# The last MLP of a hybrid trunk: down weights that change places in their buffers, a residual turned into the sums at the opening, and accumulators seeded from the sums

## The chip, the cores and the metric

The kernel runs on one core of a Trainium2 chip. Its metric is the device time in microseconds (us) of one execution, the median over several. A core has five engines with instruction queues of their own: TensorE (PE, with its weight loads PEld), VectorE (DVE), ScalarE (ACT), GpSimd (POOL) and SyncE (SP). SP and POOL here do little but issue transfers (DMA).

## The reference

A trunk of two layers on x of 512 tokens by 1024: each is a mixer and a squared-ReLU MLP, both behind an RMS norm. At the end stands one more RMS norm. The change lies in the second layer's MLP and the final norm:

```python
def rms_norm(x, gain):
    xf = x.astype(jnp.float32)
    y = xf * lax.rsqrt(jnp.mean(xf * xf, axis=-1, keepdims=True) + EPS)
    return (y * gain.astype(jnp.float32)).astype(x.dtype)
...
def sq_relu_mlp(xn, w_up, w_down):
    hid = jnp.square(jax.nn.relu(xn @ w_up))
    return hid @ w_down
```

w_up is 1024 x 4096, w_down 4096 x 1024, all in float32. The layer gives x + hid @ w_down; the kernel's output is the norm of that.

## The kernel before

**Layout.** The residual is kept transposed in xall: eight tiles xT of [128, 512], features on the partitions. Each float32 operand of a product is split in two parts of the matmul's rounded type: a high part `wh` (ACT, L104) and a low part `wl` (DVE, L107); a product is then three matmuls. Output of the down product has tokens on the partitions.

**The last MLP** is `mlp_last`. The 4096 hidden features are cut in eight blocks of 512. The first block's up product is made plainly by `up_first`, the last block's down product plainly by `row`. Between them run seven steps; step b makes the down product of block b and the up product of block b+1, each as a 2 x 2 block product with seven instead of eight multiplications. These need sums of weight quadrants and of operand quadrants, made by DVE. An up product is 24 matmuls of 128x256 (`up_product`, L1083), a down product 12 of 128x512 (`down_product`, L1094).

Five sums of down products are kept over all steps: S11, S12, SU and S21 are views of xall (1024 numbers per partition each), S5 is a tile of its own. A step computes in two-bank PSUM tiles d and e, and in four banks for the up products; results are added to the sums by DVE (L1117) or the sum is copied into the bank by ACT first (L1122) and the product accumulated on it.

**Weights of a step.** `fetch(b, name)` loads them: A1 and A2 (1 MB each, up), S1 (up, 512 KB), d11, d12, d22, dS1 and dS3 (down, 512 KB). SP issues the plain load (L1080, L134). S1, dS1, dS3 and A2 are sums of two quadrants: behind the plain load, POOL issues a second one that accumulates in flight (L1082, L1072). dS1 enters first through DVE's `d11 += ds1` at L1145, by which d11 becomes the sum for a later product; S1 through L1141.

The six 512 KB weights live in six buffers, all of the tag "comb". `step` calls `after(name)` where a weight has been used for the last time, and the next block's weight of the same name is fetched into the buffer that comes free; the names are released in the order d11, S1, d12, A1, dS3, dS1, A2, d22.

**The residual.** xall becomes the sums, so at the opening its content is written to DRAM (x_kept, 2 MB, L982). Step 0 is special ("opening"): it writes the sums rather than adding to them. In the last step, `at_the_end` reads x_kept back in four parts into freed buffers (L1222), and loads the last block's down weights as two 1 MB tiles. Then `residual(t, c)` turns 4 tiles on PE (L129), DVE adds them to a sum (L1253), ACT copies the result into an accumulator (L1257), and `row(t, c)` adds the last block's 12 matmuls (L1267), squares and sums on ACT (L1270), multiplies by the gain on DVE (L1271), and at c = 1 scales by the row's factor and writes out (L1279 to L1289).

**What sets the order.** The engines' order of instructions comes from a list scheduler in the framework, which also puts in the waits; an engine runs its list in order. SP's and POOL's lists are in order too.

Of the kernel before, what the change touches and what calls it, by code (L numbers as in the profile page):

```python
# [18 lines left out]
P = 128  # L19
D = 1024  # L20
# [30 lines left out]
def trunk_kernel(ctx: ExitStack, tc: tile.TileContext, t_in: dict, out: bass.AP):  # L51
# [7 lines left out]
    def uname(s):  # L59
        count[0] += 1  # L60
        return f"{s}_{count[0]}"
# [17 lines left out]
    def two_banks(tag):  # L79
        return psum["pool"].tile([P, 1024], F32, tag=f"ps_{tag}", bufs=1, name=uname("ps2"))  # L80
# [891 lines left out]
    def mlp_last(layer, nrm):  # L972
# [6 lines left out]
        fast = es.enter_context(tc.tile_pool(name=f"fast{layer}", bufs=1, reuse_waits="tile"))  # L979
        dram = es.enter_context(tc.tile_pool(name="spill", bufs=1, space=bass.MemoryType.DRAM))  # L980
        x_kept = dram.tile([P, ND, S], F32, name="x_kept")
        SP.dma_start(x_kept, xall)  # L982

# [6 lines left out]

        def comb():
            return fast.tile([P, 2 * S], F32, tag="comb", bufs=6, name=uname("comb"))

        def by_k(t, n):
            return t.rearrange("p (k n) -> p k n", k=n)
# [41 lines left out]
        def quadrants():  # L1037
            lead, trail = range(KH), range(KH, ND)
            quad["11"] = [nrm.parts[k][:, :, first] for k in lead]
            quad["21"] = [nrm.parts[k][:, :, first] for k in trail]  # L1040
            quad["22"] = [nrm.parts[k][:, :, second] for k in trail]
            t1, t2, t3, t4 = (by_k(comb(), KH) for _ in range(4))
# [12 lines left out]


        W = {}

# [45 lines left out]
        def step(b, q, r, after):  # L1104
            opening = b == 0
            (q11, q12), (q21, q22) = q

            def begun(src, total):
                if opening:
                    ACT.activation(total, src, AF.Copy)  # L1110
                    return two_banks("e")
# [7 lines left out]
            def onto(tag, total, a, parts):  # L1119
                t = two_banks(tag)  # L1120
                if not opening:
                    ACT.activation(t, total, AF.Copy)  # L1122
                down_product(t, a, parts, opening)
                ACT.activation(total, t, AF.Copy)
# [11 lines left out]
            down_product(d, d11, parts_of_quad(q11), True)  # L1136
            e = begun(d, S11)

# [3 lines left out]

            down_product(e, d12, parts_of_quad(q21), opening)
            add(S11, e)
# [9 lines left out]
            down_product(d, d11, parts_of_quad(q11, -1.0), False)  # L1154
            e = begun(d, S12)
            DVE.tensor_tensor(d12, d11, d12, ALU.add)
# [7 lines left out]

            down_product(e, d12, parts_of_quad(q22), opening)
            add(S12, e)
# [8 lines left out]
            down_product(d, ds3, parts_of_quad(q12), False)  # L1175
            if opening:
                ACT.activation(SU, d, AF.Copy)
            else:
                add(SU, d)
            after("dS3")  # L1180
# [8 lines left out]

            onto("e", S5, ds1, parts_of_quad(q22, -1.0))  # L1190
            after("dS1")
# [10 lines left out]
        quadrants()  # L1202
        NAMES = ("d11", "S1", "d12", "A1", "dS3", "dS1", "A2", "d22")
        for name in NAMES:
            fetch(0, name)

        kept, last = [], []

        def at_the_end(name):
            if name in ("A1", "A2"):  # L1210
                c = len(last)
                raw = load(w_dn[(NB - 1) * FB :, c * 512 : (c + 1) * 512].rearrange("(k p) n -> p k n", p=P), 4, 512)
                w = []
                for k in range(4):
                    parts = both_parts()
                    split(raw[:, k], parts[:, 0], parts[:, 1])
                    w.append((parts[:, 0], parts[:, 1]))
                last.append(w)
            elif len(kept) < ND // 2:
                t = by_k(comb(), 2)  # L1220
                i = 2 * len(kept)
                SP.dma_start(t, x_kept[:, i : i + 2])  # L1222
                kept.append(t)
            elif len(kept) == ND // 2:
                t = comb()
                SP.dma_start(t, t_in["fin_row"].to_broadcast([P, D]))
                DVE.tensor_scalar(t, t, -0.5, None, ALU.mult)
                kept.append(t)

        for b in range(NB - 1):  # L1230
            step(b, Q[b % 2], Q[(b + 1) % 2], (lambda name, b=b: fetch(b + 1, name)) if b < NB - 2 else at_the_end)


        q = Q[(NB - 1) % 2]
        DVE.tensor_tensor(S12, S12, S5, ALU.add)
        hid = {}
        for h in range(2):
            for th in range(2):
                hid[h, th] = parts_of_quad(q[h][th])
        DVE.tensor_tensor(S21, S21, SU, ALU.add)  # L1240
        DVE.tensor_tensor(SU, SU, S5, ALU.add)
        gain = kept.pop()
        place = {}
        stats = [sm(3) for _ in range(NT)]
        rows = {}

        def residual(t, c):
            src = (S11, S12, S21, SU)[2 * c + t // 2][:, t % 2 * 512 : (t % 2 + 1) * 512]
            p = bank("u")
            for j in range(4):  # L1250
                m = 4 * c + j
                tr(p[:, j * P : (j + 1) * P], kept[m // 2][:, m % 2, t * P : (t + 1) * P])
            DVE.tensor_tensor(src, p, src, ALU.subtract if c else ALU.add)  # L1253
            if t % 2 == 0:
                place["t"] = two_banks("ed"[t // 2])
            o = place["t"][:, t % 2 * 512 : (t % 2 + 1) * 512]
            ACT.activation(o, src, AF.Copy)  # L1257
            rows[t, c] = src, o

        def row(t, c):  # L1260
            y, o = rows[t, c]
            tk = slice(t % 2 * P, (t % 2 + 1) * P)
            for k in range(4):
# [6 lines left out]
            ACT.activation(sq, o, AF.Square, accum_out=stat[:, c : c + 1])  # L1270
            DVE.tensor_tensor(y, o, gain[:, c * 512 : (c + 1) * 512], ALU.mult)  # L1271
            part = stat[:, 2:3]
            if c == 0:
                DVE.tensor_scalar(part, stat[:, 0:1], 1.0 / D, EPS, ALU.mult, ALU.add)
                return
# [7 lines left out]
            y_0 = rows[t, 0][0]  # L1283
            for eng, queue, y_, cs in ((DVE, SP, y_0, slice(0, 512)), (ACT, ACT, y, slice(512, D))):
                if eng is ACT:
                    ACT.activation(y_, y_, AF.Copy, scale=r)
                else:
                    DVE.tensor_scalar(y_, y_, r, None, ALU.mult)
                queue.dma_start(out_t[:, cs], y_)  # L1289

        order = [(t, c) for c in range(2) for t in range(NT)]
        residual(*order[0])
        residual(*order[1])
        for i, tc_ in enumerate(order):
            if i + 2 < len(order):
                residual(*order[i + 2])
            row(*tc_)
        es.close()


# [547 lines left out]
```

## Time and profile before

| | us |
|---|---|
| median of 3 runs | 1097.58 |
| lowest, highest | 1096.39, 1097.94 |
| the profiled execution | 1098.03 |
| its span | 1096.3 |
| PE busy in it | 1067.1 (97%) |
| DVE busy | 871.5 (79%) |
| ACT busy | 625.7 (57%) |
| POOL busy | 75.9 (7%) |

The mean granted TensorE clock is 0.993. Times in the profile are counted from the span's start; `mlp_last`'s seven-product part fills it from about 762 us to the end. A row of the waits reads: engine and line that waited, engine and line waited for, total us, times, longest. A row of the timeline reads: start, duration, engine, line, operation, result and operands, count, and in brackets the idle time ahead of it with what ended it. A row of the windows reads: the stretch, its length, and for each engine the busy time with its count of instructions, then the granted clock, the DMA engines' share and GB/s. A row of the chain reads: start, duration, what.

### The profile page before, as it was taken

Reading aid. Unit: us, or ns where it says so; the run is one execution under the profiler, and the core shown is the slowest. Engines: PE = TensorE matmul, PEld = TensorE weight load, DVE = VectorE, ACT = ScalarE, POOL = GpSimd, SP = SyncE. Lnnn points to the kernel's source line nnn. Section 1 sums busy time; section 2 is a strip of 40 time slices with the busy share of each in tenths; the row PEclk is TensorE's granted clock in tenths of the full one; section 3 lists DMA queues with packets and bytes.
Section 4 is the critical chain, followed back from the end, with each engine's and each line's share of the span. In section 5 each row is a group of like instructions: output and inputs, shape, how many; then the busy total and the mean of one; then the engine's idle time right before and its main releaser. Section 6 shows DMA issues by size and latency. Waiting matters only on the chain.

```text
span 1096.3 us, 14765 instructions
## 1 busy us (share of the span) xinstructions
PE 1067.1 (97%) x5626; PEld 912.9 (83%) x5626; DVE 871.5 (79%) x1394; ACT 625.7 (57%) x1009; POOL 75.9 (7%) x100
## 2 busy tenths in 40 slices
PE   9999999999999999999999999999899999999976
PEld 7888888888888888888788888888789889889864
DVE  7899968987887887877694696497978988988873
ACT  7667654554453453455446545655667767667554
POOL 7210002000000000000000000001011011011000
PEclk9999999999999999999999999999999999999989
DMA  7311232232332332323213212158568679669412
GB/s 221 89 49 39 78 115 78 66 127 77 116 115 77 115 116 77 115 78 115 87 39 115 76 40 78 39 169 273 131 158 224 144 177 239 149 160 234 134 57 77
DMA packets 103430, 127.87 MB, mean 117 GB/s; under 512 B 8416, under 2 KB 74464, under 8 KB 103232
## 3 DMA queue, kind: packets, MB, share of 16 engines
q1 hardware_dynamic: 90064, 110.42, 31.5%
q0 software_dynamic: 11200, 14.68, 8.1%
q10 hardware_dynamic: 2096, 1.84, 0.5%
q8 instruction: 44, 0.72, 0.3%
q14 instruction: 26, 0.21, 0.1%
HBM read 122.47 MB, written 4.19 MB: 116 GB/s over the span
## 4 chain that ended last, share of the span: by engine, by line
PE 78%; DMA 11%; DVE 6%; ACT 2%; issue 2%; POOL 0%; DVEq 0%; SPq 0%; POOLq 0%; ACTq 0%
PE ps L112 15%; PE ps L114 15%; PE ps L113 15%; DMA comb<-in_mlp_w_down_dram 9%; PE ps L891 8%; PE ps L1092 6%; PE ps L1101 5%; PE ps L892 4%; DVE wl L107 2%; PE ps L1267 2%; PE ps L129 2%; PE ps L1492 1%; PE ps L408 1%; DMA wraw<-in_mlp_w_down_dram 1%; PE ps L1619 1%
## 5 line engine op out<-in xcount | busy, mean ns | idle before, releaser
L104 ACT ACTIVATE wh<-wraw 128x1024 fp32r<-128x1024 f32 x139 | 146.4, 1056 | 156.5 <-PE ps L113 76.4
L112 PE MATMUL ps<-set,wh 128*128 128x512 f32 x536 | 209.1, 391 | 0.5 <-ACT set L1661 0.3
L113 PE MATMUL ps<-set,wh 128*128 128x512 f32 x536 | 209.2, 391 | 0.0
L114 PE MATMUL ps<-set,wl 128*128 128x512 f32 x536 | 208.8, 390 | 0.0
L107 DVE TENSOR_TENSOR wl<-wraw,wh 128x1024 fp32r<-128x1024 f32 x139 | 169.4, 1220 | 33.2 <-ACT wh L104 33.0
L1101 PE MATMUL ps<-wh,set 128*128 128x512 f32 x392 | 129.7, 392 | 0.7 <-ACT wh L104 0.7
L104 ACT ACTIVATE wh<-comb 128x1024 fp32r<-128x1024 f32 x77 | 81.6, 1059 | 77.0 <-PE ps L891 40.9
L107 DVE TENSOR_TENSOR wl<-comb,wh 128x1024 fp32r<-128x1024 f32 x77 | 93.8, 1218 | 32.5 <-ACT wh L104 32.2
L112 PEld LDWEIGHTS ps<-set,wh 128*128 128x128 f32 x536 | 100.6, 188 | 22.3 <-ACT wh L104 1.0
L114 PEld LDWEIGHTS ps<-set,wl 128*128 128x128 f32 x536 | 100.6, 188 | 21.5 <-DVE wl L107 0.4
L113 PEld LDWEIGHTS ps<-set,wh 128*128 128x128 f32 x536 | 100.7, 188 | 19.6
L1101 PEld LDWEIGHTS ps<-wh,set 128*128 128x128 f32 x392 | 74.0, 189 | 15.3 <-ACT wh L104 0.9
L1092 PE MATMUL ps<-T,wh 128*128 128x256 f32 x448 | 79.9, 279 | 0.0
L1101 PE MATMUL ps<-wl,set 128*128 128x512 f32 x196 | 77.2, 394 | 2.0 <-DVE wl L107 2.0
L891 PE MATMUL ps<-T,wh 128*128 128x512 f32 x224 | 78.7, 391 | 0.0
L1092 PEld LDWEIGHTS ps<-T,wh 128*128 128x128 f32 x448 | 70.3, 188 | 2.2
L1092 PE MATMUL ps<-T,wl 128*128 128x256 f32 x224 | 62.5, 279 | 2.0 <-DVE wl L107 2.0
L1092 PE MATMUL ps<-set,wh 128*128 128x256 f32 x336 | 62.5, 286 | 1.5 <-ACT ps L1133 1.5
L892 PE MATMUL ps<-T,wl 128*128 128x256 f32 x224 | 63.1, 282 | 0.0
L891 PE MATMUL ps<-set,wh 128*128 128x512 f32 x168 | 60.0, 397 | 0.0
L112 PE MATMUL ps<-wh,set 128*128 128x512 f32 x144 | 58.5, 406 | 0.0
L1092 PEld LDWEIGHTS ps<-set,wh 128*128 128x128 f32 x336 | 54.3, 194 | 3.5 <-ACT ps L1133 1.9
(414 smaller groups left out, 2213.2 us busy)
## 6 DMA issues: line engine op xcount, KB each, us to landing
wraw<-in_mlp_w_up_dram SPq DMA_DIRECT2D x32, 1024.0 KB, 5.4
comb<-in_mlp_w_down_dram SPq DMA_DIRECT2D x35, 512.0 KB, 5.2
wraw<-in_gla_w_in_dram SPq DMA_DIRECT2D x12, 1024.0 KB, 5.1
wraw<-in_mlp_w_down_dram SPq DMA_DIRECT2D x11, 1024.0 KB, 5.1
raw<-in_mlp_w_down_dram SPq DMA_DIRECT2D x7, 1024.0 KB, 5.0
comb<-in_mlp_w_down_dram POOLq DMA_DIRECT2D x14, 512.0 KB, 9.6
wraw<-in_mla_w_o_dram SPq DMA_DIRECT2D x4, 1024.0 KB, 5.4
wraw<-in_gla_w_o_dram SPq DMA_DIRECT2D x4, 1024.0 KB, 5.5
```

Source lines behind the costliest of these rows:

```text
L104: order(ACT.activation(hi, src, AF.Copy))
L107: lo_eng.tensor_tensor(lo, src, f(hi), ALU.subtract)
L112: PE.matmul(psum, wh, xh, start=start, stop=False)
L113: PE.matmul(psum, wh, xl, start=False, stop=False)
L114: PE.matmul(psum, wl, xh, start=False, stop=stop)
L129: PE.transpose(psum, src, ident[: src.shape[0], : src.shape[0]])
L408: PE.matmul(p, w[:, i, j * P : (j + 1) * P], x, start=start, stop=stop)
L891: PE.matmul(o.rearrange("p (h t) -> p h t", h=2), wh, x, start=start and k == 0, stop=False, skip_group_check=True)
L892: PE.matmul(o[:, :TH], wl, x[:, 0], start=False, stop=k == KH - 1, skip_group_check=True)
L1092: PE.matmul(o, a_, x_, start=start and j == 0 and k == 0 and n == 0, stop=k == KH - 1 and n == 2, skip_group_check=True)
L1101: PE.matmul(o, x_, w_, start=start and k == 0 and n == 0, stop=k == 1 and n == 2, skip_group_check=True)
L1267: PE.matmul(o, a, b_, start=False, stop=k == 3 and n == 2, skip_group_check=True)
```

## The change

- **Buffers.** Each of the six 512 KB weights gets a home buffer, comb0 to comb5. When a weight is released, the buffer goes to another name of the next block, by the table NEXT: d11's release fetches dS1, S1's S1, d12's d11, dS3's d12, dS1's dS3, d22's d22 (A1 and A2 as before).
- **Opening.** x is not written to DRAM. `residual()` turns xall on PE into the tiles d and e, twice 16 transposes, and copies it over xall as the initial values of S11, S12, SU (negated) and S21 (with SU taken off). Step 0 is then like the others, but for S5, which starts fresh. The first block's fetches are issued in another order, S1 and dS1 first.
- **The last block.** Its down weights come as four loads of 512 KB into the buffers that d11, S1, d12 and dS3 release in the last step; `rounded(c)` splits them. S12 += S5 moves into the last step. The accumulators of the rows are seeded by ACT copies of the sums alone; the rows of c = 0 use the tiles d and e, those of c = 1 four single banks; the rows run in the order t = 2, 3, 0, 1. At c = 1 the gain and the row's factor are applied in one DVE operation; DVE's half goes out by SP's queue, ACT's by ACT's.

```diff
-        x_kept = dram.tile([P, ND, S], F32, name="x_kept")
-        SP.dma_start(x_kept, xall)
...
+        def residual():
+            def turned(tag, c, th):
+                p = two_banks(tag)
+                for t in range(2):
+                    for j in range(4):
+                        o = t * 512 + j * P
+                        src = xT[4 * c + j][:, th * TH + t * P : th * TH + (t + 1) * P]
+                        PE.matmul(p[:, o : o + P], src, ident, start=j == 0, stop=j == 3, is_transpose=True, skip_group_check=True)
+                return p
+
+            p, q = turned("d", 0, 0), turned("e", 0, 1)
+            ACT.activation(S11, p, AF.Copy)
+            ACT.activation(S12, q, AF.Copy)
+            p, q = turned("d", 1, 1), turned("e", 1, 0)
+            ACT.activation(SU, p, AF.Copy, scale=-1.0)
+            DVE.scalar_tensor_tensor(S21, q, -1.0, SU, ALU.mult, ALU.subtract)
...
+        home = {"S1": 0, "dS1": 1, "d11": 2, "d12": 3, "dS3": 4, "d22": 5}
...
-            W[name] = t = by_k(comb(), KH if name == "S1" else 2)
+            W[name] = t = by_k(comb(home[name]), KH if name == "S1" else 2)
...
-        for name in NAMES:
+        residual()
+        for name in ("S1", "dS1", "d11", "A1", "d12", "dS3", "A2", "d22"):
             fetch(0, name)
+        NEXT = {"d11": "dS1", "S1": "S1", "d12": "d11", "A1": "A1", "dS3": "d12", "dS1": "dS3", "A2": "A2", "d22": "d22"}
...
+            if name in ("d11", "S1", "d12", "dS3"):
+                i = len(last_raw)
+                t = by_k(comb(home[name]), 2)
+                k0 = (NB - 1) * FB + i % 2 * 256
+                SP.dma_start(t, w_dn[k0 : k0 + 256, i // 2 * 512 : (i // 2 + 1) * 512].rearrange("(k p) n -> p k n", p=P))
+                last_raw.append(t)
+            if name == "dS1":
+                DVE.tensor_tensor(S12, S12, S5, ALU.add)
...
+                new = NEXT[name]
+                if name in home:
+                    home[new] = old[name]
+                fetch(b + 1, new)
...
+        for c in range(2):
+            for th in (1, 0):
+                total = (S11, S12, S21, SU)[2 * c + th]
+                if c == 0:
+                    o = two_banks("de"[th])
+                    ACT.activation(o, total, AF.Copy)
+                for i in range(2):
+                    cs = slice(i * 512, (i + 1) * 512)
+                    if c:
+                        o = bank("u")
+                        ACT.activation(o, total[:, cs], AF.Copy, scale=-1.0)
+                    rows[2 * th + i, c] = total[:, cs], o if c else o[:, cs]
...
-            tr(p[:, j * P : (j + 1) * P], kept[m // 2][:, m % 2, t * P : (t + 1) * P])
-            DVE.tensor_tensor(src, p, src, ALU.subtract if c else ALU.add)
...
+            DVE.scalar_tensor_tensor(y, o, r, gain[:, 512:], ALU.mult, ALU.mult)
+            SP.dma_start(out_t[:, 512:], y)
+            ACT.activation(y_0, y_0, AF.Copy, scale=r)
+            ACT.dma_start(out_t[:, :512], y_0)
```

The order shows three places. First SP's queue, the fetches that step 0 issues for block 1. Before, the eight rows are d11, S1, d12, A1, dS3, dS1, A2, d22:

```order
L1080 DMA comb_1375_7243<-in_mlp_w_down_dram 128x2x512
L1080 DMA comb_1380_7276<-in_mlp_w_up_dram 128x4x256
L1080 DMA comb_1383_7298<-in_mlp_w_down_dram 128x2x512
L134 DMA wraw_1388_7333<-in_mlp_w_up_dram 128x8x256
L1080 DMA comb_1391_7354<-in_mlp_w_down_dram 128x2x512
L1080 DMA comb_1400_7413<-in_mlp_w_down_dram 128x2x512
L134 DMA wraw_1404_7448<-in_mlp_w_up_dram 128x8x256
L1080 DMA comb_1408_7471<-in_mlp_w_down_dram 128x2x512
```

After, at the same places, they are dS1, S1, d11, A1, d12, dS3, A2, d22:

```order
L1096 DMA comb_1379_7279<-in_mlp_w_down_dram 128x2x512
L1096 DMA comb_1384_7313<-in_mlp_w_up_dram 128x4x256
L1096 DMA comb_1387_7335<-in_mlp_w_down_dram 128x2x512
L134 DMA wraw_1392_7370<-in_mlp_w_up_dram 128x8x256
L1096 DMA comb_1395_7391<-in_mlp_w_down_dram 128x2x512
L1096 DMA comb_1404_7449<-in_mlp_w_down_dram 128x2x512
L134 DMA wraw_1408_7484<-in_mlp_w_up_dram 128x8x256
L1096 DMA comb_1412_7508<-in_mlp_w_down_dram 128x2x512
```

The rows look alike, since a buffer's name says nothing of what is in it: the fetch of dS1 moved from the sixth row to the first, and d11's, d12's and dS3's moved back to the third, the fifth and the sixth. POOL's accumulating loads follow, dS1's now ahead of S1's. PE, DVE and ACT have the same instructions in the same order in steps 1 to 6.

Second, ACT at the opening, behind the first block's squares (the two rows set<-tmp). Before comes d12's high part at once, then y's copy and S11's:

```order
L1033 ACTIVATE set_1303_6866<-tmp_1339_7025 128x256
L104 ACTIVATE wh_1367_7171<-comb_1350_7070 128x1024
L1133 ACTIVATE ps_1359_7114<-ps_1356_7085 128x512
L104 ACTIVATE set_1308_6871<-set_1301_6864 128x512
L1110 ACTIVATE xT_73<-ps2_1360_7116 128x1024
```

After, the three copies of the turned residual stand ahead:

```order
L1030 ACTIVATE set_1303_6862<-tmp_1339_7021 128x256
L1065 ACTIVATE xT_73<-ps2_1348_7061 128x1024
L1066 ACTIVATE xT_73<-ps2_1349_7070 128x1024
L1068 ACTIVATE xT_73<-ps2_1350_7081 128x1024
L104 ACTIVATE wh_1371_7207<-comb_1356_7111 128x1024
L1145 ACTIVATE ps_1363_7150<-ps_1360_7121 128x512
L104 ACTIVATE set_1308_6867<-set_1301_6860 128x512
L1125 ACTIVATE ps2_1367_7171<-ps2_1364_7152 128x1024
```

The copies of d12's high part, of y and of the first product (L1110 before, L1125 after) keep their order among each other, three copies later. On PE two groups of eight transposes stand ahead of the first up product, and two more behind its first eight matmuls.

Third, PE behind the last step's last product (its last row is the first below). Before:

```order
L1101 MATMUL ps2_1731_9813<-wh_1732_9815,set_1309_6872 128x512
L129 MATMUL ps_1740_9855<-ident_64,comb_1693_9581 128x128 x2
L129 MATMUL ps_1740_9855<-ident_64,comb_1698_9614 128x128 x2
L129 MATMUL ps_1741_9862<-ident_64,comb_1693_9581 128x128 x2
L129 MATMUL ps_1741_9862<-ident_64,comb_1698_9614 128x128 x2
L129 MATMUL ps_1744_9886<-ident_64,comb_1693_9581 128x128 x2
```

After, the same place in the list:

```order
L1117 MATMUL ps2_1729_9834<-wh_1730_9836,set_1309_6868 128x512
L1284 MATMUL ps2_1740_9880<-set_1722_9788,set_1312_6871 128x512 x2
L1284 MATMUL ps2_1740_9880<-set_1722_9788,set_1313_6872 128x512
L1284 MATMUL ps2_1740_9880<-set_1723_9791,set_1312_6871 128x512 x2
L1284 MATMUL ps2_1740_9880<-set_1723_9791,set_1313_6872 128x512
L1284 MATMUL ps2_1740_9880<-set_1724_9794,set_1314_6873 128x512 x2
L1284 MATMUL ps2_1740_9880<-set_1724_9794,set_1315_6874 128x512
```

The transposes of the kept residual are gone from here, and the matmuls of the first row follow the product directly.

More of the change, by code (lines that the diff above doesn't have):

```diff
@@ L1041, in quadrants @@
             quad["22"] = [nrm.parts[k][:, :, second] for k in trail]
-            t1, t2, t3, t4 = (by_k(comb(), KH) for _ in range(4))
+            t1, t2, t3, t4 = (by_k(comb(i), KH) for i in range(2, 6))
             for k in lead:
@@ L1117, in add, with onto @@
                 DVE.tensor_tensor(total, t, total, ALU.add)
[L1119 removed]
+            def onto(tag, total, a, parts, fresh=False):
                 t = two_banks(tag)
[L1121 removed]
+                if not fresh:
                     ACT.activation(t, total, AF.Copy)
[L1123 removed]
+                down_product(t, a, parts, fresh)
                 ACT.activation(total, t, AF.Copy)
@@ L1163, in step @@
             after("S1")
-            down_product(e, d12, parts_of_quad(q22), opening)
+            down_product(e, d12, parts_of_quad(q22), False)
             add(S12, e)
@@ L1175, in step @@
             down_product(d, ds3, parts_of_quad(q12), False)
[L1176 to L1179, printed above, removed]
+            add(SU, d)
             after("dS3")
@@ L1215, in at_the_end, with rounded @@
+        last_raw, last, gain = [], [[], []], []
+        def rounded(c):
+            for i in range(2):
+                raw = last_raw[2 * c + i]
+                for k in range(2):
                     parts = both_parts()
                     split(raw[:, k], parts[:, 0], parts[:, 1])
[L1217 to L1225, printed above, removed]
+                    last[c].append((parts[:, 0], parts[:, 1]))
@@ L1226, in at_the_end, with after @@
                 SP.dma_start(t, t_in["fin_row"].to_broadcast([P, D]))
-                DVE.tensor_scalar(t, t, -0.5, None, ALU.mult)
-                kept.append(t)
+                gain.append(t)
+                rounded(0)
         for b in range(NB - 1):
-            step(b, Q[b % 2], Q[(b + 1) % 2], (lambda name, b=b: fetch(b + 1, name)) if b < NB - 2 else at_the_end)
+            final = b == NB - 2
+            old = dict(home)
+            def after(name, b=b, final=final, old=old):
+                if final:
+                    return at_the_end(name)
+                new = NEXT[name]
+                if name in home:
+                    home[new] = old[name]
+                fetch(b + 1, new)
@@ L1234, in mlp_last @@
+            step(b, Q[b % 2], Q[(b + 1) % 2], after)
         q = Q[(NB - 1) % 2]
-        DVE.tensor_tensor(S12, S12, S5, ALU.add)
         hid = {}
-        for h in range(2):
-            for th in range(2):
-                hid[h, th] = parts_of_quad(q[h][th])
+        for h, th in ((0, 0), (0, 1), (1, 1), (1, 0)):
+            hid[h, th] = parts_of_quad(q[h][th])
         DVE.tensor_tensor(S21, S21, SU, ALU.add)
         DVE.tensor_tensor(SU, SU, S5, ALU.add)
-        gain = kept.pop()
-        place = {}
+        rounded(1)
@@ L1244, in mlp_last @@
+        gain = gain[0]
+        DVE.tensor_scalar(gain, gain, -0.5, None, ALU.mult)
         stats = [sm(3) for _ in range(NT)]
         rows = {}
[L1247 to L1251, printed above, removed]
-                tr(p[:, j * P : (j + 1) * P], kept[m // 2][:, m % 2, t * P : (t + 1) * P])
[L1253 to L1258, printed above, removed]
+        for c in range(2):
[4 more added lines that the diff above has]
+                    ACT.activation(o, total, AF.Copy)
+                for i in range(2):
+                    cs = slice(i * 512, (i + 1) * 512)
[3 more added lines that the diff above has]
+                    rows[2 * th + i, c] = total[:, cs], o if c else o[:, cs]
@@ L1283, in row @@
             y_0 = rows[t, 0][0]
[L1284 to L1297, printed above, removed]
+            DVE.scalar_tensor_tensor(y, o, r, gain[:, 512:], ALU.mult, ALU.mult)
+            SP.dma_start(out_t[:, 512:], y)
+            ACT.activation(y_0, y_0, AF.Copy, scale=r)
+            ACT.dma_start(out_t[:, :512], y_0)
+        for c in range(2):
+            for t in (2, 3, 0, 1):
+                row(t, c)
         es.close()
```

32 lines of the change are left out of this document (10 added, 22 removed).

## The prediction

> **What bounds the kernel now.** I read the page first: the busy shares and the chain that ended last.
> ```profile
> PE 1067.1 (97%) x5626; PEld 912.9 (83%) x5626; DVE 871.5 (79%) x1394; ACT 625.7 (57%) x1009; POOL 75.9 (7%) x100
> ...
> PE 78%; DMA 11%; DVE 6%; ACT 2%; issue 2%; POOL 0%; DVEq 0%; SPq 0%; POOLq 0%; ACTq 0%
> ```
> TensorE (PE) is the bound. Yet 11% of the chain is DMA, in a kernel whose PE is 97% busy, so some transfers end last. The waits inside the part that changes (740 to 1100 us) say where, PE's first, then the largest one of VectorE (DVE):
> ```profile
> PE ps L1092 <- DVE wl L107: 9.7, 7, 2.5
> PE ps L129 <- DVE xT L1253: 2.9, 2, 2.3
> PE ps L1101 <- DVE wl L107: 2.0, 1, 2.0
> PE ps L1267 <- DVE xT L1271: 1.9, 1, 1.9
> PE ps L1092 <- ACT ps L1133: 1.5, 1, 1.5
> PE ps L1267 <- ACT ps L1257: 1.4, 2, 1.1
> PE ps L1101 <- ACT wh L104: 0.7, 1, 0.7
> ```
> ```profile
> DVE comb L1145 <- DMA comb<-in_mlp_w_down_dram: 21.1, 7, 5.7
> ```
> Seven times, once per step, PE waits for a rounded weight part that DVE makes late, and seven times DVE waits at L1145, where dS1 is added to d11. The chain between two such waits names the owner:
> ```profile
> 993.50 9.66 DMA comb<-in_mlp_w_down_dram
> ...
> 1003.72 0.85 POOL comb L1082
> ...
> 1005.06 9.74 DMA comb<-in_mlp_w_down_dram
> ...
> 1016.03 2.35 DVE wl L107 x2
> ```
> dS1 is a plain load of 9.66 us and then an accumulating one of 9.74 us, with POOL between: about 21 us from its buffer's release. Its own old buffer is released late in a step (after the product onto S5), and it is wanted first of all sums in the next.
>
> The stages, cut at PE's stalls (the opening, seven steps, the turn to the last block, its rows, the end):
> ```profile
> 762.50:775.18 12.68, 9.18 (x63) 8.12 (x61) 9.44 (x11) 6.66 (x9) 1.28 (x1) 1.00 0.50 86
> ...
> 775.18:814.17 38.99, 36.46 (x228) 32.82 (x229) 29.66 (x34) 27.70 (x36) 4.95 (x4) 1.00 0.76 189
> 814.17:855.50 41.33, 40.82 (x252) 37.06 (x252) 35.06 (x39) 26.79 (x34) 4.95 (x4) 0.96 0.71 179
> 855.50:895.43 39.93, 39.30 (x253) 35.67 (x253) 34.89 (x39) 28.41 (x36) 4.95 (x4) 1.00 0.74 185
> 895.43:935.96 40.53, 39.29 (x252) 35.65 (x253) 34.89 (x39) 28.90 (x37) 4.95 (x4) 1.00 0.74 182
> 935.96:977.03 41.07, 39.31 (x253) 35.67 (x253) 34.88 (x39) 28.84 (x36) 4.98 (x4) 1.00 0.72 180
> 977.03:1017.31 40.28, 39.30 (x252) 35.65 (x253) 34.89 (x39) 27.51 (x35) 4.95 (x4) 1.00 0.73 183
> 1017.31:1054.25 36.94, 34.27 (x218) 30.79 (x219) 33.31 (x41) 24.82 (x36) 0.00 (x0) 1.00 0.39 129
> 1054.25:1060.50 6.25, 3.36 (x22) 2.72 (x20) 6.25 (x9) 2.85 (x5) 0.00 (x0) 0.79 0.00 0
> 1060.50:1089.80 29.30, 26.04 (x106) 20.01 (x104) 10.54 (x28) 11.58 (x30) 0.00 (x0) 0.93 0.13 50
> 1089.80:1096.30 6.50, 0.00 (x0) 0.00 (x0) 1.62 (x5) 1.90 (x5) 0.00 (x0) 0.67 0.27 101
> ```
> Columns: length, PE, weight load, DVE, ACT, POOL, granted clock. Within a step PE loses only its one stall, length less busy: 2.53, 0.51, 0.63, 1.24, 1.76, 0.98. The turn (6.25 us, PE half idle) and the rows (29.30 us) are loose too.
>
> What a product costs without a stall, from the chain in mid-step (an up product on a quadrant, a down product, an up product on one of the sums T):
> ```profile
> 952.70 2.87 PE ps L1092 x24
> 955.58 2.75 PE ps L1101 x12
> 958.32 2.80 PE ps L1092 x24
> ```
> A step has seven down products and seven up products. Four of these, on T, at 2.80, three at 2.87: 7 x 2.75 + 3 x 2.87 + 4 x 2.80 = 39.06 us.
>
> **The change, part by part.** *The six full steps.* Each engine's order of instructions in steps 1 to 6 stays; only what is loaded into which buffer changes. dS1 now follows d11's release, the first of a step, S1 stays in its own, d11 follows d12, d12 follows dS3, dS3 follows dS1. The loads' places now, in the fifth step (d11's, then dS3's and dS1's in one row):
> ```profile
> 942.80 0.37 SPq L1080 DMA_DIRECT2D comb<-in_mlp_w_down_dram  x1
> ...
> 952.42 6.13 SPq L1080 DMA_DIRECT2D comb<-in_mlp_w_down_dram  x2
> ```
> So dS1, which needs some 21 us, starts where d11 starts now, at 942.80, and lands near 964; it is wanted at 971.6, where DVE begins to idle (974.61 less 3.05, in the row of L1145 below). d11 becomes a plain load one down product later, and d12 starts where dS3 does, at 952.42, a plain load too, wanted after d11. dS3 starts last, where dS1 does now, and has nearly half a step more until its product. I take the L1145 wait as gone, and the PE stall with it: 2.53 + 0.51 + 0.63 + 1.24 + 1.76 + 0.98 = 7.65. Is something else late next? DVE's own supply: where it waited, it idled longer than PE did.
> ```profile
> 974.61 1.23 DVE L1145 TENSOR_TENSOR comb<-comb,comb 128x1024 f32<-128x1024 f32 x1 [3.05 <-DMA comb<-in_mlp_w_down_dram]
> ```
> 3.05 of DVE against PE's 1.76 in that step leaves DVE 1.29 us of slack a step, so the stall goes wholly. Two smaller gains: the restart after a stall (39.30 busy against 39.06 unstalled, 0.24 x 6 = 1.4) and step 1's slow stretch, 40.82 - 39.30 = 1.52, where the clock was halved after the 2.53 us stall:
> ```profile
> 816.00:818.00 2.00, 2.00 (x12) 2.00 (x11) 2.00 (x3) 0.04 (x1) 0.00 (x0) 0.50 0.00 0
> 1062.00:1064.00 2.00, 2.00 (x6) 1.58 (x5) 0.06 (x1) 0.00 (x0) 0.00 (x0) 0.50 0.00 0
> ```
> Together 10.5, of the bounds 0 (rival 2) to 10.6 (all of it). The Trainium skill, "TensorE: Matmul & The Clock Gate", Part 1, has the clock halved only after at least one idle window of about 3.4 us; by that rule stalls of 2.53 and 2.3 us would have cost no clock, and the saving would be smaller by the 1.5 here and some 2 in the tail. The rows show the half clock behind both, so the trace decides: these microseconds are there to be had.
>
> *The opening (762.5 to 775.18).* The spill of 2 MB leaves the queue, so the first fetches start sooner. Two stalls stand here now, 1.5 (y's copy behind late work on ACT) and the one below; PE's idle time is 12.68 - 9.18 = 3.50. They go with dS1's wait, but 32 transposes and four copies come, before and inside the first product:
> ```profile
> 775.18 0.38 PE L1092 MATMUL ps<-T,wl 128*128 128x256 f32 x1 [2.04 <-DVE wl L107]
> ```
> ```profile
> 701.76 1.03 PE L129 MATMUL ps<-ident,g 128*128 128x128 f32 x8
> ```
> ```profile
> 770.17 1.00 ACT L1110 ACTIVATE xT<-ps 128x1024 f32<-128x1024 f32 x1
> ```
> Eight transposes last 0.9 to 1.03, so 32 are 3.6 to 4.1 us of PE. I chain them by hand: transposes 762.5 to 764.3; copies S11 and S12 (1.0 each) to 766.4, with z's first half under them; the second sixteen, into the same two-bank tiles, 765.5 to 767.4; SU and S21 to 769.8 under z's rest; d12's high part, then y's copy, to 770.1; the d11 product to 772.1; its copy, T2's high part, its low part at 775.4. So the matmul that started at 775.18 starts at about 775.45: a loss of 0.3. Bounds: the 3.50 filled with 32 x 0.1, a gain of 0.3; all of today's idle time kept on top of the transposes, a loss of 3.5. I take the chain's value, near the gain's end, since dS1's lateness is what made both stalls.
>
> *The last step (1017.31 to 1054.25).* Unstalled its PE work up to there is 36.94 less the stalls 0.72 and 1.96, four transposes 0.45 and the restart and slow share (34.27 busy against products of 6 x 2.75 + 2.87 x 22/24 + 2.87 + 4 x 2.80 = 33.2): 3.7 possible. The weights of the last block now come as four 512 KB loads into released buffers; today ACT waits for them:
> ```profile
> 1039.98 2.19 ACT L104 ACTIVATE set<-wraw 128x512 fp32r<-128x512 f32 x4 [3.62 <-DMA wraw<-in_mlp_w_down_dram]
> ```
> Their rounding now stands elsewhere, the first half ahead of the v copy of the last steps' products, and I count 1.1 us of a new wait of PE there (half of that row's 2.19). Gain 2.6, bounds 0.5 to 3.7.
>
> *Turn and rows (1054.25 to 1096.3: 42.05 us).* The reads of the spill, 28 transposes, and the sums' add behind them (L1253) leave; the accumulators are seeded straight from the sums. What must remain: 8 rows of 12 matmuls at 2.75, 22.0; the end 6.50; and row (1,0), which reuses the tile of row (0,0) and waits for its Square and multiplication by the gain, about 0.6, near the 0.69 that a DVE operation of that size takes. I add 0.1 for the first row. 29.2, so 12.8 saved, about 2.1 of it (29.30 x 0.07, by the clock of 0.93) the half clock behind the 2.3 us stall. Bounds 10 (a wait of 2.8 stays) to 13.4.
>
> Sum: -0.3 + 10.5 + 2.6 + 12.8 = 25.6. The span goes from 1096.3 to 1070.7; with the 1.73 us around it (1098.03) the profiled run to 1072.4. The median shown is 0.45 below the profiled run: 1072.
>
> **The rivals.** *1. The transposes slow the clock.* Thirty-two in a row of small bursts could lower the granted clock as the idle stretches do; price as in step 1, 1.5 to 1.7: 1073.7. For it: the window with twelve transposes (1054.25) has clock 0.79, though 2.9 us of idle lie in it. Against: the eight at 701.76 ran at the usual pace. 0.22. The Trainium skill, same page, Part 4, says that transposes do not count as busy for the gate; a burst of eight is too short to decide that.
>
> *2. The steps gain nothing,* because DVE's in-order supply (34.9 busy of 39.1) hits another late weight, d11 or d12, in the same place. Then 10.5 stay: 1082.5. Against: the slack of 1.29 and plain loads of 4 us. 0.10.
>
> *3. The rows wait as now,* for rounded hidden parts and seeds in place of transposes: the 2.9 + 1.9 + 1.4 of waits and the 2.1 of clock stay: 1080.3. Against: the first rows' sums lack nothing but S5 at the last step's end, and that addition moves up into the step. 0.08.
>
> *4. Slower: the fetches collide.* dS1 and S1 now accumulate at once beside d11, d12 and A1, early in the step. A1 is the one that would show:
> ```profile
> 950.69 0.37 SPq L134 DMA_DIRECT2D wraw<-in_mlp_w_up_dram  x1
> ```
> ```profile
> wraw<-in_mlp_w_up_dram SPq DMA_DIRECT2D x1, 1024.0 KB, 8.3
> ```
> ```profile
> 965.41 1.05 ACT L104 ACTIVATE wh<-wraw 128x1024 fp32r<-128x1024 f32 x1
> ```
> It lands at 959.0, 6.4 us before its use. To lose, PE must stall more than 25.6 / 6 = 4.3 us a step, so A1 must take over 8.3 + 6.4 + 4.3 = 19 us. At such a price, say 6 us a step, 1108. 0.04.
>
> *5. The opening keeps its stalls,* +3.2: 1075.5. 0.04.
>
> **How the numbers follow.** The forecast (0.52) gives 1072, with its own range of 1068.5 (opening +0.6, last step +1.1, tail +0.6, restart and drain 1.2) to 1075. Rivals 1 and 5 lie inside; rival 3 and most of 2 are taken in by 1082. A measurement here tells about 0.2%, 2.2 us, from no change. All but rival 4 are faster by more than that: 0.95 faster, 0.01 the same, 0.04 slower.
>
> **What would show it.** Right: no DVE wait at L1145's place for a down weight, PE stalls in steps near zero, steps 39.1 long, clock 1.00 from the opening to the end; no transposes behind 1030; the rows within about 23 us. Wrong: a DMA named at another addition of a step (d11 or d12 late), A1 landing later than its rounding, a clock under 1.00 in the 5 us behind the opening's transposes, or PE waiting for a seed's copy at the rows.

## The result, and the profile after

The changed kernel takes 1069.49 us (median of 4, 1068.75 to 1070.06) against 1096.99 for the kernel before: a ratio of 0.9749, with a 95% interval of 0.9732 to 0.9766. The forecast was 1072, range 1068 to 1082.

The page of the profiled execution (1070.06 us, span 1068.4): busy shares, then the chain that ended last by engine.

```profile
PE 1058.9 (99%) x5626; PEld 908.2 (85%) x5626; DVE 868.1 (81%) x1384; ACT 630.2 (59%) x1010; POOL 78.5 (7%) x100
...
PE 93%; DVE 3%; ACT 2%; DMA 1%; issue 1%; ACTq 0%; DVEq 0%
```

DMA's share of the chain fell from 11% to 1%. PE's waits between 740 and 1100 us are these two, all of them:

```profile
PE ps L1108 <- DVE wl L107: 0.5, 1, 0.5
PE ps L1061 <- ACT xT L1065: 0.4, 1, 0.4
```

The stages, cut as before (the opening from the first transposes to the third matmul on T2; the steps to the third matmul of the last step's second up product; the last step; the rows; the end):

```profile
761.33:774.92 13.59, 12.65 (x95) 11.68 (x93) 10.57 (x12) 9.53 (x12) 1.28 (x1) 1.00 0.26 40
774.92:1006.47 231.55, 231.55 (x1489) 210.89 (x1490) 206.52 (x226) 167.86 (x210) 29.99 (x24) 1.00 0.75 191
1006.47:1039.66 33.19, 33.19 (x217) 30.23 (x215) 32.98 (x41) 26.96 (x37) 0.00 (x0) 1.00 0.24 80
1039.66:1062.00 22.34, 22.33 (x97) 17.61 (x95) 9.99 (x24) 13.09 (x30) 0.00 (x0) 1.00 0.13 48
1062.00:1068.40 6.40, 0.00 (x0) 0.00 (x0) 1.48 (x5) 1.97 (x6) 0.00 (x0) 0.78 0.44 164
```

PE is busy for the whole of the steps, of the last step and, but for 0.01 us, of the rows. In the first four stretches the clock is 1.00. Against the kernel before:

| stage | before, us | after, us | gain | forecast |
|---|---|---|---|---|
| up to the opening | 762.51 | 761.33 | 1.2 | 0 |
| opening | 12.67 | 13.59 | -0.9 | -0.3 |
| steps | 242.13 | 231.55 | 10.6 | 10.5 |
| last step | 36.94 | 33.19 | 3.75 | 2.6 |
| turn, rows, end | 42.05 | 28.74 | 13.3 | 12.8 |

The first row is not the change's: the kernels below, whose work up to there is that of one of these two, reach the place between 760.25 and 761.12, those with the old opening as early as those with the new one.

### The profile page after: what moved, and what is told of

It is laid out like the page before. It is cut to its first block, busy times and chain, and to the rows that moved or that the text cites. A ratio compares the mean times of both kernels' runs of the same rounds, so it can differ in the third digit from the quotient of the medians.

```text
span 1068.4 us, 14750 instructions
## 1 busy us (share of the span) xinstructions
PE 1058.9 (99%) x5626; PEld 908.2 (85%) x5626; DVE 868.1 (81%) x1384; ACT 630.2 (59%) x1010; POOL 78.5 (7%) x100
## 4 chain that ended last, share of the span: by engine, by line
PE 93%; DVE 3%; ACT 2%; DMA 1%; issue 1%; ACTq 0%; DVEq 0%
PE ps L112 15%; PE ps L114 15%; PE ps L113 15%; PE ps L1108 13%; PE ps L1117 13%; PE ps L891 8%; PE ps L892 4%; PE ps L1504 2%; PE ps L129 1%; PE ps L1284 1%; PE ps L408 1%; DMA comb<-in_mlp_w_down_dram 1%; PE ps L1631 1%; DVE wl L107 1%; DVE T L999 0%
## 5 line engine op out<-in xcount | busy, mean ns | idle before, releaser
L1117 PE MATMUL ps<-wh,set 128*128 128x512 f32 x392 | 129.3, 390 | 0.0
L112 PEld LDWEIGHTS ps<-set,wh 128*128 128x128 f32 x536 | 100.6, 188 | 22.2 <-ACT wh L104 1.0
L113 PEld LDWEIGHTS ps<-set,wh 128*128 128x128 f32 x536 | 100.7, 188 | 19.7
L112 PE MATMUL ps<-wh,set 128*128 128x512 f32 x144 | 58.6, 407 | 0.0
L114 PE MATMUL ps<-wh,set 128*128 128x512 f32 x144 | 56.8, 396 | 0.0
```

The lines of the kernel that those rows point to most:

```text
L112: PE.matmul(psum, wh, xh, start=start, stop=False)
L113: PE.matmul(psum, wh, xl, start=False, stop=False)
L114: PE.matmul(psum, wl, xh, start=False, stop=stop)
L1117: PE.matmul(o, x_, w_, start=start and k == 0 and n == 0, stop=k == 1 and n == 2, skip_group_check=True)
```

## The experiments

Each kernel ran beside the kernel before, whose medians were 1096.99 to 1097.97 us.

**One half each.** *rot_only* is the kernel before with the change of buffers and the fetch order of the first block alone:

```diff
-            W[name] = t = by_k(comb(), KH if name == "S1" else 2)
+            W[name] = t = by_k(comb(home[name]), KH if name == "S1" else 2)
...
+                new = NEXT[name]
+                if name in home:
+                    home[new] = old[name]
+                fetch(b + 1, new)
```

> The kernel before, with the buffers' change of places and the first block's fetch order alone; spill, special opening and tail stay. Theory (dS1's late landing is what PE waits for in the steps): no wait at the addition of dS1, the six stalls, their restarts and the slow stretch go (10.5 us), and most of the opening's 3.5 us of stalls with them: 1097.0 - 13.5 = 1083.5, between 1082.5 and 1087. The tail stays at 42 us. Rival (the steps gain because the spill and the 2 MB of reads leave the queue, not by the places): within 3 us of before.

Measured: 1079.61 (1078.82 to 1080.23), ratio 0.9846 [0.9814, 0.9878]: 4 us better than the theory's figure and below its range. PE's waits in it are the opening's last one and those of the old tail:

```profile
PE ps L129 <- DVE xT L1266: 3.4, 2, 2.3
PE ps L1280 <- DVE xT L1284: 1.9, 1, 1.9
PE ps L1280 <- ACT ps L1270: 1.4, 2, 1.1
PE ps L1094 <- DVE wl L107: 0.5, 1, 0.5
```

```profile
769.99:1035.31 265.32, 265.32 (x1706) 241.51 (x1707) 237.29 (x264) 193.75 (x246) 29.97 (x24) 1.00 0.71 185
1035.31:1041.60 6.29, 2.89 (x21) 2.42 (x20) 6.29 (x9) 2.85 (x5) 0.00 (x0) 0.91 0.00 0
```

The first row is all steps to the last product's end: 265.32 us, PE busy throughout, against 279.07 before and 264.74 in the changed kernel (the difference is four transposes, 0.60 by their row). So the last step's stalls went too, with the old 1 MB loads in place: ACT's wait for them, 3.62 us in the row that the prediction shows, is 0.39 here. Moving dS1 is enough for the 3.75 us booked there. The opening took 9.40 us (760.59 to 769.99) against 13.59 with the transposes.

*own_buffers* is the changed kernel with each weight in its own buffer:

```diff
-        NEXT = {"d11": "dS1", "S1": "S1", "d12": "d11", "A1": "A1", "dS3": "d12", "dS1": "dS3", "A2": "A2", "d22": "d22"}
+        NEXT = {n: n for n in ("d11", "S1", "d12", "A1", "dS3", "dS1", "A2", "d22")}
```

> The changed kernel, but each weight keeps its own buffer as before. Theory: DVE waits for dS1's load again, once a step, 1.8 to 4 us, PE 0.5 to 2.5 each, and the clock falls behind the longest: 1069.5 + 10.5 = 1080, between 1077 and 1082. Opening and tail stay as in the changed kernel (tail 28.7 us). Rival (the spill's traffic was the cause): within 2 us of the changed kernel.

Measured: 1078.62 (1076.73 to 1078.91), ratio 0.9834 [0.9807, 0.9862], as the theory said. The stall is back:

```profile
PE ps L1108 <- DVE wl L107: 5.4, 5, 2.4
```

The opening (13.28 us) and the tail (28.63) are near the changed kernel's. The steps and the last step, from the windows:

```profile
773.82:1012.79 238.97, 234.09 (x1489) 212.55 (x1489) 205.48 (x225) 168.28 (x211) 29.75 (x24) 0.99 0.74 185
1012.79:1046.37 33.58, 33.55 (x215) 30.26 (x215) 33.42 (x41) 25.87 (x36) 0.00 (x0) 1.00 0.23 79
```

The steps take 7.4 us longer than in the changed kernel. This profiled execution is the fastest of its four (1076.73); by the medians 9.1 us are lost. The last step has no stall of PE, though dS1 comes late in the steps: without the reads of x_kept and with the four early loads, the last step runs without its stalls too. So the tail's gain and the steps' are separate, the spill is not what stalls the steps, and the last step's 3.75 us can be had in two ways: by dS1's place, or by the new last block.

**Does the place in the queue matter, or the release?** *ds1_from_ds3* is the changed kernel with the smallest exchange:

```diff
+        NEXT = {"d11": "d11", "S1": "S1", "d12": "d12", "A1": "A1", "dS3": "dS1", "dS1": "dS3", "A2": "A2", "d22": "d22"}
```

> The changed kernel with the smallest change of places: only dS1 and dS3 swap (dS3's release fetches dS1, dS1's fetches dS3). dS1's load starts where d12's does in the changed kernel, 10.6 us later than there; with 9.3 us for the plain load, 1.5 to issue and 9 for the accumulating one it lands 20 us later, near DVE's want, 0.6 us late, which DVE's slack of 1.29 us swallows. Theory: within 1 us of the changed kernel, 1069.5 to 1070.5. Rival (every down weight has to move up): 3 us or more above it.

Measured: 1069.29 (1068.92 to 1069.39), no different from the changed kernel. Of the four new places, exchanging dS1 and dS3 is enough.

That exchange also puts dS1 ahead of dS3 in POOL's queue, where the accumulating loads are issued. A second reading of the old trace belongs here: in the chain quoted in the prediction, the plain load of 9.66 us is dS3's, not dS1's (it starts at 993.50, and dS3's load is issued one step of 41.07 us earlier at 952.42). dS1's own plain load, issued at 958.19, took 4.9 us. POOL issues both accumulating loads one behind the other (the next two rows: POOL's timeline and the transfers it issues, in the kernel before):

```profile
962.26 2.54 POOL L1082 DMA_DIRECT2D comb<-in_mlp_w_down_dram  x2 [10.97 <-DMA comb<-in_mlp_w_down_dram]
```

```profile
comb<-in_mlp_w_down_dram POOLq DMA_DIRECT2D x2, 512.0 KB, 10.2
```

*ds3_plain* takes dS3's accumulating load out of the kernel before, so that one quadrant is missing in that sum:

```diff
-                "S1": ((1, 1), (1, 0)), "dS1": ((1, 1), (1, 0)), "dS3": ((1, 0), (0, 0)),
+                "S1": ((1, 1), (1, 0)), "dS1": ((1, 1), (1, 0)), "dS3": ((1, 0), None),
```

> The kernel before without dS3's accumulating load, so one quadrant of the weights is left out of that sum. It takes dS3's load out of POOL's queue ahead of dS1's and 0.5 MB out of the traffic; dS1's release stays. Theory (release too late): dS1 lands 0.5 to 2 us sooner, the stalls shrink, 3 to 7 us gained, 1090 to 1094. Rival (dS1's accumulating load is held up in POOL's queue behind dS3's): stalls go, 1084 to 1087.

Measured: 1080.78 (1079.47 to 1081.61), ratio 0.9857 [0.9829, 0.9884]. The rival had it, with 3 us more than its range, since the last step's stalls and a part of the opening's went too: the steps ran as in rot_only (265.29 us from 770.69 to 1035.98) though dS1's buffer is released as late as before. But this also took traffic away. *ds1_first* leaves traffic and releases alone and only turns the two loads round in POOL's queue:

```diff
             SP.dma_start(t, q(b, *plain))
-            if more:
+            if name == "dS1" and b:
+                s = W["dS3"][:, 0, :1]
+                z0 = sm(1)
+                POOL.tensor_scalar(z0, t[:, 0, :1], 0.0, None, ALU.mult)
+                POOL.tensor_tensor(s, s, z0, ALU.add)
+            if more and not (name == "dS3" and b):
                 POOL.dma_start(t, q(b, *more), accum_op=ALU.add)
+            if name == "dS1" and b:
+                POOL.dma_start(W["dS3"], q(b, 0, 0), accum_op=ALU.add)
```

> The kernel before, all releases and all traffic as they are, but POOL issues dS1's accumulating load ahead of dS3's (two tiny POOL operations make dS3's wait for dS1's plain load; values unchanged). Theory formed on ds3_plain (dS1's accumulating load stands behind dS3's in the queue): the steps run without stalls as with dS3's load left out, 1080 to 1083. Rival (dS1's buffer is released too late, or the sheer traffic): stalls stay, 1092 or more.

Measured: 1084.63 (1083.37 to 1085.07), ratio 0.9886 [0.9871, 0.99]: 12.9 us gained, without any stall of PE in the steps or in the last step:

```profile
774.16:1041.04 266.88, 266.88 (x1707) 242.90 (x1707) 237.79 (x264) 193.66 (x245) 36.56 (x36) 0.99 0.72 184
```

The theory's range (1080 to 1083) was too low, since the opening keeps its two stalls here, 1.91 and 2.04 us. One step, POOL's rows, then the transfer issued at 957.12, then DVE's addition:

```profile
955.65 0.91 POOL L1084 TENSOR_SCALAR sm<-comb 128x1 f32<-128x1 f32 x1 [12.16 <-DMA comb<-in_mlp_w_down_dram]
956.65 0.18 POOL L1085 TENSOR_TENSOR comb<-comb,sm 128x1 f32<-128x1 f32 x1
957.12 1.25 POOL L1087 DMA_DIRECT2D comb<-in_mlp_w_down_dram  x1 [0.29 <-DVE tmp L1194]
```

```profile
comb<-in_mlp_w_down_dram POOLq DMA_DIRECT2D x1, 512.0 KB, 7.9
```

```profile
965.08 1.23 DVE L1152 TENSOR_TENSOR comb<-comb,comb 128x1024 f32<-128x1024 f32 x1 [0.45 <-DMA comb<-in_mlp_w_down_dram]
```

Ahead of dS3's, dS1's accumulating load takes 7.9 us and DVE waits 0.45; behind it the pair took 10.2 (dS3's 9.6, dS1's 10.9) and DVE waited 3.05. From the plain load's issue to DVE's start that is 13.8 us (951.26 to 965.08) against 16.4 (958.19 to 974.61), and PE has no wait left. The late release alone is just bearable; the late release and the place behind dS3 together are not. Whether an early release would do with dS1 still behind dS3 was not run.

*ds3_behind* was meant as the same test without the POOL operations: in the kernel before, `fetch` does nothing at dS3's release and fetches dS1 and dS3 at dS1's.

```diff
+            if b and name == "dS3":
+                return
+            if b and name == "dS1":
+                fetch_one(b, "dS1")
+                return fetch_one(b, "dS3")
```

> The kernel before, each weight in its own buffer, with both loads of dS3 issued only behind dS1's. dS1's release is as late as before. Queue theory: 1080 to 1083, dS3 itself has half a step to land. Rival (release too late): 1092 or more; rival (traffic): the load of dS3 moved into the crowded stretch makes it 1097 or more.

Measured: 1083.99 (1083.17 to 1085.15). It does not tell what it was made for: the six old buffers are handed out in turn, so with the new order dS1 got the buffer that dS3 releases, and its load started there (944.55 in a step whose dS1 release is at 950). It is ds1_from_ds3 on the kernel before, and confirms that run. *own_ds3_behind* tried it on the changed kernel with fixed buffers:

```diff
+        NEXT = {n: n for n in ("d11", "S1", "d12", "A1", "dS3", "dS1", "A2", "d22")}
...
+                if new != "dS3":
+                    fetch(b + 1, new)
+                if new == "dS1":
+                    fetch(b + 1, "dS3")
```

> The changed kernel without any change of buffers: each weight keeps its own, and dS3's two loads are issued behind dS1's. Queue theory: the order in POOL's queue is all that the steps need, so within 1.5 us of the changed kernel, 1069 to 1071. Rival (the early release of dS1's buffer is needed): stalls as in own_buffers, 1077 or more.

Measured: 1079.03 (1075.97 to 1080.64), with stalls of 0.81 to 1.83 us in six steps. Neither theory is touched: by the issue times the scheduler put dS3's loads ahead of dS1's again (one SP row of two at 951.82, as at 952.42 in the kernel before), so this is own_buffers once more.

**The opening.** *no_residual* leaves the 32 transposes and their four copies out (x enters the sums unturned):

```diff
-        residual()
         for name in ("S1", "dS1", "d11", "A1", "d12", "dS3", "A2", "d22"):
```

> The changed kernel without the opening's 32 transposes and four copies: x stays as it lies, so the residual is added untransposed and the output differs by that. By the opening of rot_only, which has no transposes (9.4 us against 13.6): 1069.5 - 4.2 = 1065.3, between 1064.5 and 1066.5. Rival (the transposes lie in time that PE would wait for dS1 anyway): 1068 or more.

Measured: 1065.74 (1065.43 to 1066.08): the transposes cost 3.75 us, nearly the 3.92 that their two rows show in the changed kernel:

```profile
761.33 1.91 PE L1061 MATMUL ps<-ident,xT 128*128 128x128 f32 x16
764.61 2.01 PE L1061 MATMUL ps<-ident,xT 128*128 128x128 f32 x16 [0.41 <-ACT xT L1065]
```

They are on the path in full; what paid for them in the opening was dS1's earlier arrival (rot_only's 9.40 us).

*many_turns* makes each of them four times into the same place:

```diff
-                for t in range(2):
+                for t in [0, 1] * 4:
```

> The changed kernel with each of the opening's 32 transposes made four times into the same place, so PE does nothing but transposes for about 8 us, then eight matmuls, then 8 us again. If transposes do not keep the clock up, the granted clock falls to 0.5 within some 4 us of them and the products behind start slow: 1069.5 + 12 + 2 to 5. If they count, it stays at 1.00: 96 more at 0.12 us, 1069.5 + 11.5 = 1081.

Measured: 1079.46 (1079.37 and 1079.54), 9.97 us for 96 more, 0.104 each. PE ran transposes alone for twice 7.2 us. The clock is full through the end of the second burst, which ends at 775.9, and behind it:

```profile
760.65 7.15 PE L1061 MATMUL ps<-ident,xT 128*128 128x128 f32 x64
768.70 7.21 PE L1061 MATMUL ps<-ident,xT 128*128 128x128 f32 x64
```

```profile
773.00:775.00 2.00, 2.00 (x21) 2.00 (x20) 0.00 (x0) 0.00 (x0) 0.00 (x0) 1.00 0.00 0
775.00:777.00 2.00, 2.00 (x20) 2.00 (x19) 0.21 (x1) 1.03 (x1) 0.00 (x0) 1.00 0.00 0
777.00:779.00 2.00, 2.00 (x13) 1.78 (x13) 1.18 (x2) 1.27 (x2) 0.00 (x0) 1.00 0.04 8
```

Here transposes keep a full clock up; whether they bring a halved one back was not run.

**The last step's loads.** *two_loads* puts back the last block's weights as two loads of 1 MB:

```diff
-            if name in ("d11", "S1", "d12", "dS3"):
+            if name in ("A1", "A2"):
+                c = len(last_raw)
+                last_raw.append(load(w_dn[(NB - 1) * FB :, c * 512 : (c + 1) * 512].rearrange("(k p) n -> p k n", p=P), 4, 512))
```

> The changed kernel with the last block's down weights loaded as before, two of 1 MB behind A1 and A2. By the prediction's term for the last step (four early loads save 2.6 us): 1072. By rot_only, whose last step ran without stalls with the old loads: within 1 us of the changed kernel, 1069 to 1070.5.

Measured: 1070.01 (1069.74 to 1070.15), 0.5 us above the changed kernel, within what a measurement tells. With dS1 early, the four early loads add nothing; with dS1 late, as in own_buffers, the last step runs without a stall with them.

**DVE's slack.** *slow_dve* was to load DVE:

```diff
+            for _ in range(4):
+                DVE.tensor_scalar(ds1, ds1, 1.0, None, ALU.mult)
             DVE.tensor_tensor(d11, ds1, d11, ALU.add)
```

> The changed kernel with four more DVE operations a step (dS1 multiplied by 1.0 in place, 0.69 us each, 2.8 us a step). By the slack of 1.29 us a step that the prediction read: 1.5 us of stall in each of six steps, 1069.5 + 9 = 1078.5, between 1076 and 1082. Rival (all of DVE's idle time, 39.06 - 34.9 = 4.2 us a step, can be used): 1070.5 or less.

Measured: 1098.68 (1094.55 to 1100.78), 29 us worse, which neither figure foresaw. The scheduler put the first of these operations some 23 us ahead of the addition (921.09 and 944.02 in one step), into the step before, where that dS1 has not landed yet:

```profile
PE ps L1108 <- DVE wl L107: 20.1, 6, 4.6
```

```profile
DVE comb L1158 <- DMA comb<-in_mlp_w_down_dram: 31.8, 6, 6.8
```

So it is no test of the slack. It shows the old fault made again, and larger: an in-order engine that touches a weight too early. *dve_work* has the load without the early touch:

```diff
             DVE.tensor_tensor(d11, ds1, d11, ALU.add)
+            for _ in range(4):
+                DVE.tensor_tensor(tmp(), d11[:, 0], d11[:, 1], ALU.add)
```

> The changed kernel with four idle DVE additions a step (128x512, 0.69 us each, into scratch, needing nothing but d11's sum, so no transfer is waited for earlier). By the slack of 1.29 us a step that the prediction read from the stall: 2.76 - 1.29 = 1.5 us a step, six steps, 1069.5 + 9 = 1078.5, between 1076 and 1081, a little more if the clock falls behind a stall. Rival (the slack is larger than the stall showed, up to 4.2 us): 1069 to 1071.

Measured: 1073.89 (1073.56 to 1074.39), 4.4 us worse. Seven steps with 2.76 us more each cost 0.63 a step. PE's wait is 0.38 of it, so some 2.4 us of DVE's time a step were free, between the 1.29 of the theory and the 4.2 of the rival. Half of the 4.4 us stands in PE's waits, below; the other half is PE's busy time, 39.33 us a step against 39.06 in the changed kernel, near the 0.24 that the prediction gives a restart:

```profile
PE ps L1117 <- DVE wl L107: 2.2, 6, 0.4
PE ps L1108 <- DVE wl L107: 0.5, 1, 0.5
```

No kernel here with the same output beats the changed one; ds1_from_ds3 equals it with two buffers exchanged in place of four moved.

## Why the prediction was right, point by point

- **Steps, 10.5 forecast, 10.6 measured.** That DVE's wait for dS1 at L1145 is what PE waits for held: rot_only, own_buffers and ds1_first agree. The account of why dS1 is late was wrong in one step, "dS1 is a plain load of 9.66 us and then an accumulating one": the 9.66 us are dS3's load, and dS1 is late by its release together with its place behind dS3 in POOL's queue. From dS1's own issue to DVE's addition it is 16.4 us, not some 21. ds1_first removes the stalls without an earlier release. The prediction spoke of a release where a queue's order would have been enough; that the early release also put dS1 ahead of dS3 in that queue was not in its account, so the size came out partly by luck. (dS1 is also not the first sum wanted: DVE reads S1 before it, at 969.75 against 974.61.)
- **Opening, -0.3 forecast, -0.9 measured.** Mis-sized by 0.6, most of it behind the first down product. The chain made by hand has the product's end 9.6 us behind the opening's start, measured 9.76, and T2's low part 3.35 behind that, measured 3.83: ACT first rounds another operand there (0.63 us at 771.09), which the chain left out. PE's two waits are 0.41 us for the copy of S11 and 0.53 for T2's low part. The bounds (0.3 to -3.5) held.
- **Last step, 2.6 forecast, 3.75 measured.** The forecast took the 3.7 possible, gave them to the four loads, and took off a new wait of 1.1. There is no new wait (PE is busy for 33.19 of 33.19 us). The four loads were only half of the cause: rot_only, ds1_first and two_loads have the gain by dS1's place alone, own_buffers has it with the new last block alone. How a late dS1 delays the old load was not followed; its transfer took 7.9 us in the kernel before. Each engine's order is the same through step 5 only; in the last step DVE and ACT round the last block's weights in other places.
- **Tail, 12.8 forecast, 13.3 measured.** The rows follow each other without a wait; the 0.6 us for row (1,0) and the 0.1 for the first row were not needed. The rows' matmuls are mixed: ACT's Squares start at 1042.58, 1047.47 and 1048.21, not one row of 2.75 us apart. own_buffers and rot_only show that the tail's gain is the new tail's; no run takes its parts (reads, transposes, additions) one by one.
- **The clock.** The slow stretches went with the stalls, as the trace of before had it. Rival 1 (transposes slow the clock) fell: 1.00 in the opening and in many_turns. The Trainium skill, "TensorE: Matmul & The Clock Gate", Part 4, which says that transposes do not count as busy for the gate, is not borne out by these runs.
- **The other rivals.** Rival 2 (DVE's supply becomes the bound) fell with PE's waits, and dve_work shows some 2.4 us of slack. Rivals 3 and 5 fell with the list of PE's waits (rival 5's price is a slip: 1072 + 3.2 is 1075.2, not 1075.5). Rival 4 (fetches collide) fell: DVE and ACT wait for no weight in the steps of the changed kernel.

The forecast was 2.5 us too high: 0.6 too little loss at the opening, against 1.15 in the last step, 0.5 in the tail, 0.1 in the steps and 1.2 ahead of the opening. No part of the change explains these 1.2 us; they are luck.

## What to carry to other kernels

Where a transfer ends last, ask first what stands ahead of it in the queue of the engine that issues it: here two accumulating loads in the wrong order cost 13 us, and exchanging the two buffers was worth as much as moving all four. When the operand of an in-order engine moves, look at its first reader in that engine's real order, which a scheduler may set far from where the code stands. PE time that can't be hidden (32 transposes, 3.75 us) is worth paying when it replaces a stage in which PE waits and then runs slow.

## What the runs showed of the hardware

Behind short idle stretches of PE the granted clock fell to half. In rot_only the last product of the rows started after 1.85 us of idle, and the two stretches of 2 us behind it ran at 0.70 and 0.50; in own_buffers 2.4 us of idle gave 0.72 and 0.50:

```profile
1066.90 4.61 PE L1280 MATMUL ps<-set,set 128*128 128x512 f32 x12 [1.85 <-DVE xT L1284]
```

```profile
1066.90:1068.90 2.00, 2.00 (x6) 1.64 (x7) 0.88 (x4) 0.93 (x2) 0.00 (x0) 0.70 0.71 262
1068.90:1070.90 2.00, 2.00 (x6) 1.55 (x5) 0.00 (x0) 0.00 (x0) 0.00 (x0) 0.50 0.71 262
```

Those 12 matmuls took 4.61 us, against 2.75 at full clock. Every stall of 2.2 us or more in these traces was followed by such a stretch; of those between 1.7 and 2.05 us some were (2.04 in ds1_first, 1.83 in own_ds3_behind) and some were not (2.04 and 1.76 in the kernel before). A stall of PE can thus cost twice its own length: here 1.85 us of idle and 1.86 of slower matmuls.
